# S5 branch of a hybrid stream step: real scans in a turning frame, and tables and coefficients made during the first projection

## The chip, the cores and the metric

One core of a Trainium2 chip runs the whole program. The metric is the device time of one execution in microseconds (us). The engines are PE (TensorE matmuls; PEld is its weight load), DVE (VectorE), ACT (ScalarE), POOL (GpSimd) and SP (SyncE, which here only issues DMAs; ACT issues DMAs too).

## The reference, cut to what matters

The kernel is one inference step of a two-layer encoder over a prompt of 16 + 2048 frames and 8 running streams of 16 frames. The part that the change touches is the S5 mixer of layer 0: 32 groups of 64 complex states, a diagonal recurrence, then a gelu and a gated linear unit (GLU).

```python
dt = jnp.exp(log_dt)[:, None]
mag = jnp.exp(lam_re * dt)
ab_re, ab_im = mag * jnp.cos(lam_im * dt), mag * jnp.sin(lam_im * dt)
...
bu_re = jnp.einsum('btgc,gpc->btgp', ug, bb_re)     # and bu_im
_, _, h_re, h_im = lax.associative_scan(_cplx_combine, (a_re, a_im, bu_re, bu_im), axis=1)
y = einsum(h_re, c_re) - einsum(h_im, c_im)
y = gelu(y.reshape(bsz, T, W_A) + d * uf)
y = y * jax.nn.sigmoid(y @ w_glu + b_glu)
```

The rest of layer 0 is an input projection `u @ ev_w_in`, a causal convolution with SiLU, an mLSTM and an output projection; layer 1 has its own projections, a retention and an RG-LRU.

## The kernel before, in words

All matmuls of the projections are done as three products of split operands (`mm3`, L109 to L113), since each fp32 operand is held as a high and a low part (`split`, L103: an ACT cast, then a DVE or POOL subtraction). The code is plain Python over tiles; a planner puts every engine's instructions into one order ahead of time. It goes by program order, but lets a later instruction pass an earlier one that is not ready. On the chip each engine then runs its list strictly in that order. A tile of a pool takes its buffers in program order among the tiles of the same name, and must wait until the last reader of the buffer's former tile is done; pools on the right side form a stack, so that a pool that is opened after another one is closed gets the same addresses, and its tiles wait for the last use of the tiles that lay there.

The phases follow one another:

- `phase_in0`: six token blocks `seq = (2, 3, 4, 5, 0, 1)`, each with 8 output tiles of 128 columns: 4 for the S5 input (`uas`) and 4 for its gate (`zst`). Small work is set between the blocks: after block i = 0 the parameters, after i = 1 `prep_ml` and `s5_open` (powers of the S5 transition, `s5pw`, and the coefficients `s5bp`, `s5b0`, `s5b1`, in the pools `s5keep` and `s5kb`), after i = 4 the first weights of the next phase (`w_first`: tiles `wfh` and `wfl`, opened on the right side after `s5kb`). Then `uas` goes to DRAM (`e.ua`).
- `phase_l0`: three thirds of the tokens. A third has for each of 8 slices m an x tile (matmul, ACT copy to `xb`, four convolution passes on DVE (L537, L539), SiLU (L408), later a small gate matmul `pg` (L414) into one accumulator, m = 0 first) and a z tile (SiLU only, L382). The first x tile of the first third, and it alone, takes its weights from `w_first`. After every second slice `values` makes the value rows (`vo`, L439). The generator `s5` is advanced by one step after each tile from the third on; in the last third the z tiles come after S5 has been run to its end.
- `s5`: per q of 8 (4 groups each) load `s5u`, make the coefficient tile `s5ba` (L690 to L695), transpose it and multiply (`s5ee`, the input of the recurrence, 129 chunks per group). Then the recurrence over the chunks: `advance` on odd chunks (L751 to L755), 64 dependent steps of five small operations (L764 to L768), `advance` again. Then `s5y`, per q: the output coefficients `s5ca` (L816 to L820, a third of it on POOL), a Toeplitz block `s5tz` that goes through DRAM (`s5kp`, L830 and L833) and the output matmuls (L844 to L848). Once the last third has begun (`loaded`), `s5g`: load the result `s5gy` from DRAM (L874, 32 DMAs), gelu (L876), and 8 GLU blocks.
- then `phase_mlstm`, `phase_out0`, and layer 1 in `phase_in1` and `phase_ret`.

The names that count below: the pool `s5kb` is closed in `s5` after the recurrence (L783), so that `w_first`, `s5a` and the rest lie below it.

Of the kernel before, what the change touches and what calls it, by code (L numbers as in the profile page):

```python
# [19 lines left out]
NSEQ = 8  # L20
# [182 lines left out]
def phase_in0(e):  # L203
# [6 lines left out]
    with P(e, "a_w") as wp, P(e, "a_sb", 2) as sb, PS(e, "a_ps") as ps:  # L210
# [37 lines left out]
        for i, bi in enumerate(seq):  # L248
# [306 lines left out]
def s5_open(e, ps):  # L555
# [5 lines left out]
    with P(e, "s5prm", side="right") as sb:  # L561
# [37 lines left out]
        pw = s5.pw = keep.tile([128, 2, G, 17], F32, name="s5pw")  # L599
# [4 lines left out]
        t1 = sb.tile([128, G, 16], F32, name="s5t1")  # L604
        t2 = sb.tile([128, G, 16], F32, name="s5t2")
        k = 1
        while k < 16:
# [24 lines left out]
        sh = [128, G, 16]  # L632
        cmul(v, dk[:, 0], dk[:, 1], (pw[:, 0, :, 0:16], pw[:, 1, :, 0:16]),
             (kap[:, 0, :, None].to_broadcast(sh), kap[:, 1, :, None].to_broadcast(sh)), t1, t2)
# [21 lines left out]
        for q in range(2):  # L656
            hr = sb.tile([128, 128], F32, name=f"s5hr{q}")
# [9 lines left out]
def s5_u(e, sb, q):  # L667

    ur = sb.tile([128, 2, 4, NCH], F32, name="s5u")
# [6 lines left out]
def s5(e, ps):  # L676
# [6 lines left out]
    with P(e, "s5a", side="right") as sb:  # L683
        for q in range(8):
            gs = slice(4 * q, 4 * q + 4)
            ur = s5_u(e, sb, q)
            ba = sb.tile([128, 4, 16, 16], F32, name="s5ba")
            tmp = sb.tile([128, 4, 16, 16], F32, name="s5tm")
            sh = [128, 4, 16, 16]
            v.tensor_tensor(ba, p.bp[:, 0, gs, :, None].to_broadcast(sh), p.b[0][:, gs, None, :].to_broadcast(sh),  # L690
                            op=OP.mult)
            v.tensor_tensor(tmp, p.bp[:, 1, gs, :, None].to_broadcast(sh), p.b[1][:, gs, None, :].to_broadcast(sh),
                            op=OP.mult)
            v.tensor_add(ba, ba, tmp)
            v.tensor_copy(p.bb[:, gs, :], ba[:, :, 15, :])  # L695
# [37 lines left out]
        yield  # L733

        a32 = sb.tile([128, 2, G], F32, name="s5a32")
        a1 = sb.tile([128, G], F32, name="s5c1", bufs=2)
        a2 = sb.tile([128, G], F32, name="s5c2", bufs=2)
        v.tensor_mul(a1, p.a16[:, 0], p.a16[:, 0])
        v.tensor_mul(a2, p.a16[:, 1], p.a16[:, 1])
        v.tensor_sub(a32[:, 0], a1, a2)  # L740
        v.scalar_tensor_tensor(a32[:, 1], p.a16[:, 0], 2.0, p.a16[:, 1], op0=OP.mult, op1=OP.mult)

        def advance(dst, src, n, g0):

            gs = slice(g0, g0 + G // 2)
            h = ee[:, gs, src:src + 2 * n - 1:2]
            d = ee[:, gs, dst:dst + 2 * n - 1:2]
            t1 = sb.tile([128, G // 2, n], F32, name="s5ba")
            t2 = sb.tile([128, G // 2, n], F32, name="s5tm")
            bc = lambda j, ph: p.a16[ph, j, gs, None].to_broadcast([h[ph].shape[0], G // 2, n])  # L750
            v.tensor_tensor(t2[UP], h[LO], bc(1, LO), op=OP.mult)  # L751
            v.tensor_tensor(t2[LO], h[UP], bc(1, UP), op=OP.mult)
            nc.gpsimd.tensor_tensor(t1, h, bc(0, slice(0, 128)), op=OP.mult)
            v.tensor_add(d, d, t2)
            v.tensor_add(d, d, t1)  # L755

        for g0 in (0, G // 2):
            advance(2, 1, PCH // 2, g0)
            yield
        for c in range(2, PCH + 1, 2):  # L760
            a1 = sb.tile([128, G], F32, name="s5c1", bufs=2)
            a2 = sb.tile([128, G], F32, name="s5c2", bufs=2)
            h = ee[:, :, c - 2]
# [19 lines left out]
    cls(e, "s5kb")  # L783
    with P(e, "s5y", side="right") as sb:

        pw = p.pw
        cp = sb.tile([128, 2, G, 17], F32, name="s5cp")
        v.tensor_copy(cp[UP, 0], pw[UP, 0])
        v.tensor_scalar(cp[LO, 0], pw[LO, 1], -1.0, None, op0=OP.mult)
        v.tensor_scalar(cp[UP, 1], pw[UP, 1], -1.0, None, op0=OP.mult)  # L790
        v.tensor_scalar(cp[LO, 1], pw[LO, 0], -1.0, None, op0=OP.mult)
# [1262 lines left out]
```

## Time and profile before

| | us |
|---|---|
| three runs | 3146.6, 3149.01, 3157.82 |
| median | 3149.01 |
| the profiled execution, its own time | 3155.99 |
| its span from the first to the last instruction | 3154.3 |
| PE busy in the span | 3008.8 (95%) |
| DVE busy | 1722.9 (55%) |
| ACT busy | 1058.0 (34%) |
| POOL busy | 902.6 (29%) |

All views below are of the profiled execution, with times counted from the start of its span. A view by stretches gives the busy time of each engine in a stretch; PEclk in it is the granted TensorE clock as a share of 2.4 GHz. A view of waits adds up the idle time of an engine before instructions of a line, under the name of what ended last. The timeline lists instructions with start and duration, and in brackets the idle time of the engine ahead of them.

### The profile page before, as it was taken

The numbers are of one execution on the slowest core, as the hardware profiler recorded it, in microseconds if no ns is written. First come the engines' busy times: TensorE is split into PE (matmuls) and PEld (weight loads), VectorE is DVE, ScalarE is ACT, GpSimd is POOL, SyncE is SP. The second block draws the span as 40 slices with busy tenths as digits, with TensorE's granted clock in tenths as the row PEclk, the third lists the DMA queues.
The fourth block names the chain that finished last, engine by engine and source line by source line (L and its number), as shares of the span: only waits on it lengthen the run. The fifth ranks groups of instructions, "written<-read, shape, count | busy, mean of one in ns | idle before, by whom it ended". The sixth has DMA issues, their size and how long they took to land.

```text
span 3154.3 us, 45102 instructions
## 1 busy us (share of the span) xinstructions
PE 3008.8 (95%) x17435; PEld 2721.3 (86%) x17435; DVE 1722.9 (55%) x3449; ACT 1058.0 (34%) x1860; POOL 902.6 (29%) x931
## 2 busy tenths in 40 slices
PE   8999978997999899999999999999999999999999
PEld 8999877997987787766799999999998897888887
DVE  4236797465446886143355666766620026665664
ACT  4223332335343343211224555555531112211221
POOL 6103424343325663111202111111110014433432
PEclk9999988998999999999999999999999999999999
DMA  6436433558453556755532111111122148544442
GB/s 213 117 84 202 127 117 115 156 166 178 145 156 119 160 153 181 232 187 172 157 132 73 51 51 51 50 49 49 47 83 76 52 152 247 141 119 133 137 124 74
DMA packets 444033, 396.35 MB, mean 126 GB/s; under 512 B 43401, under 2 KB 392785, under 8 KB 443818
## 3 DMA queue, kind: packets, MB, share of 16 engines
q1 hardware_dynamic: 333164, 268.13, 29.8%
q10 hardware_dynamic: 110654, 125.33, 11.9%
q8 instruction: 137, 2.24, 0.3%
q14 instruction: 78, 0.64, 0.1%
HBM read 262.12 MB, written 131.27 MB: 125 GB/s over the span
## 4 chain that ended last, share of the span: by engine, by line
PE 75%; DVE 15%; DMA 5%; issue 3%; ACT 2%; POOL 1%; SPq 0%; ACTq 0%; DVEq 0%; POOLq 0%
PE p_pm L112 8%; PE p_pm L113 8%; PE p_pm L111 8%; PE pm L111 4%; PE pm L112 4%; PE pm L113 4%; PE r_pm L112 4%; PE r_pm L113 4%; PE r_pm L111 4%; PE pa L111 3%; PE pa L112 3%; PE pa L113 3%; DVE p_d L1637 1%; DVE xc L539 1%; DMA m_rw<-d_grow 1%
## 5 line engine op out<-in xcount | busy, mean ns | idle before, releaser
L111 PE MATMUL p_pm<-pu,p_wh 128*128 128x384 f32 (+1 forms) x1568 | 512.1, 327 | 0.2 <-ACT pu L105 0.2
L112 PE MATMUL p_pm<-pu,p_wh 128*128 128x384 f32 (+1 forms) x1568 | 511.8, 327 | 0.0
L113 PE MATMUL p_pm<-pu,p_wl 128*128 128x384 f32 (+1 forms) x1568 | 511.3, 326 | 0.0
L111 PE MATMUL pm<-ub,wh 128*128 128x384 f32 (+1 forms) x1136 | 382.8, 338 | 12.7 <-ACT vo L439 9.8
L112 PE MATMUL pm<-ub,wh 128*128 128x384 f32 (+1 forms) x1136 | 381.0, 335 | 1.6 <-DVE ub L106 1.6
L113 PE MATMUL pm<-ub,wl 128*128 128x384 f32 (+1 forms) x1136 | 376.8, 335 | 0.0
L111 PEld LDWEIGHTS p_pm<-pu,p_wh 128*128 128x128 f32 x1568 | 294.2, 188 | 1.8 <-issue 1.2
L112 PEld LDWEIGHTS p_pm<-pu,p_wh 128*128 128x128 f32 x1568 | 294.6, 188 | 1.0 <-issue 0.8
L113 PEld LDWEIGHTS p_pm<-pu,p_wl 128*128 128x128 f32 x1568 | 294.5, 188 | 0.0
L111 PEld LDWEIGHTS pm<-ub,wh 128*128 128x128 f32 x1136 | 219.1, 193 | 18.6 <-ACT vo L439 10.3
L112 PE MATMUL r_pm<-rol,r_gh 128*128 128x512 f32 x544 | 218.1, 401 | 5.0 <-POOL rol L106 5.0
L112 PEld LDWEIGHTS pm<-ub,wh 128*128 128x128 f32 x1136 | 219.6, 193 | 3.0 <-DVE ub L106 2.1
L113 PEld LDWEIGHTS pm<-ub,wl 128*128 128x128 f32 x1136 | 218.7, 193 | 1.2 <-issue 1.1
L111 PE MATMUL r_pm<-roh,r_gh 128*128 128x512 f32 x544 | 217.7, 401 | 0.7 <-ACT p_o L1547 0.7
L113 PE MATMUL r_pm<-roh,r_gl 128*128 128x512 f32 x544 | 217.4, 400 | 0.8 <-DVE r_gl L106 0.8
L106 POOL TENSOR_TENSOR p_wl<-p_wr,p_wh 128x1024 fp32r<-128x1024 f32 x34 | 81.8, 2408 | 384.9 <-ACT p_wh L105 384.9
L106 POOL TENSOR_TENSOR wl<-wr,wh 128x1024 fp32r<-128x1024 f32 x47 | 120.3, 2560 | 246.5 <-ACT wh L105 217.5
L112 PEld LDWEIGHTS r_pm<-rol,r_gh 128*128 128x128 f32 x544 | 103.0, 189 | 25.3 <-POOL rol L106 5.4
L113 PEld LDWEIGHTS r_pm<-roh,r_gl 128*128 128x128 f32 x544 | 103.1, 189 | 22.6 <-DVE r_gl L106 1.3
L111 PEld LDWEIGHTS r_pm<-roh,r_gh 128*128 128x128 f32 x544 | 102.6, 189 | 21.8 <-ACT p_o L1547 1.2
L106 POOL TENSOR_TENSOR p_xcl<-p_xc,p_xch 128x384 fp32r<-128x384 f32 (+1 forms) x48 | 47.2, 982 | 245.3 <-ACT p_xch L105 209.3
L1637 DVE RECIPROCAL p_d<-p_d 128x384 f32<-128x384 f32 (+1 forms) x48 | 116.7, 2430 | 0.6
(716 smaller groups left out, 6805.7 us busy)
## 6 DMA issues: line engine op xcount, KB each, us to landing
wr<-in_ev_w_in_dram SPq DMA_DIRECT2D x47, 512.0 KB
p_wr<-in_od_w_in_dram SPq DMA_DIRECT2D x40, 512.0 KB
d_in<-p_o ACTq DMA_DIRECT2D x80, 192.0 KB
m_rw<-d_grow SPq DMA_DIRECT2D x18, 512.0 KB
s5u<-d_ua SPq DMA_DIRECT2D x32, 274.0 KB
d_v<-vo ACTq DMA_DIRECT2D x68, 128.0 KB
m_va<-d_v SPq DMA_DIRECT2D x17, 512.0 KB
d_h<-o_x ACTq DMA_DIRECT2D x17, 512.0 KB
```

What stands on the lines that cost most here:

```text
L106: (nc.gpsimd if pool else nc.vector).tensor_tensor(l, x, h, op=OP.subtract)
L111: nc.tensor.matmul(out, a[0], b[0], start=start, stop=False, **kw)
L112: nc.tensor.matmul(out, a[0], b[1], start=False, stop=False, **kw)
L113: nc.tensor.matmul(out, a[1], b[0], start=False, stop=stop, **kw)
L539: v.scalar_tensor_tensor(out, x(j), pc[:, m, cw + j:cw + j + 1], out, op0=OP.mult, op1=OP.add)
L1637: v.reciprocal(d[:, :n], d[:, :n])
```

## The change

The recurrence over chunks is complex: state times `a16` (a 16th power) plus input. The change turns the input of each chunk c by the phase of `a16` to the power -c, runs a real scan with the magnitude `m16` for each of the 32 groups, and turns the result back. For that it makes per group a table of 128 phases (`e.rot`) by repeated squaring (`s5_phasors`, 10 squarings of 10 operations) and doubling (`s5_coef`). The coefficient tiles `s5ba` and `s5ca` are made there too. Table and coefficients go to DRAM and are loaded back one step ahead of their use. `s5_coef` runs its first part (tables, `s5ba`) after block i = 2 of `phase_in0` and its second part (C coefficients, `s5ca`) after i = 3, where it also closes `s5kb`. The pool `w_first` is opened at i = 4 as before. `s5pw` moves from `s5keep` to `s5kb`. The 64 chunk steps, both `advance` passes and the coefficient work inside `s5` are gone. The loads of `s5gy` get a step of their own, ahead of the GLU weights and of gelu, and the operands of GLU block b + 1 are made ahead of the matmuls of block b. The generator has 10 steps before the output part instead of 17, and 3 GLU blocks instead of one are left for the run to the end.

```diff
                 s5_open(e, ps)
+                coef = s5_coef(e, ps)
+            if i in (2, 3):
+                next(coef)
             if i == 4:
                 fp = opn(e, "w_first", side="right")
...
-        pw = s5.pw = keep.tile([128, 2, G, 17], F32, name="s5pw")
+        s5_phasors(v, sb, kb, s5, csn, sn, mag, keep)
+        pw = s5.pw = kb.tile([128, 2, G, 17], F32, name="s5pw")
...
+def s5_phasors(v, sb, kb, s5, cs, sn, mag, keep):
...
+    pp = s5.pp = kb.tile([128, 2, ROT, G], F32, name="s5pp")
...
+    def square(oc, os_, c, s):
+        v.tensor_mul(t1, c, c)
+        v.tensor_mul(t2, s, s)
+        v.scalar_tensor_tensor(os_, c, 2.0, s, op0=OP.mult, op1=OP.mult)
+        v.tensor_sub(oc, t1, t2)
+        v.tensor_mul(t1, oc, oc)
+        v.tensor_mul(t2, os_, os_)
+        v.tensor_add(t1, t1, t2)
+        v.tensor_scalar(t1, t1, -0.5, 1.5, op0=OP.mult, op1=OP.add)
+        v.tensor_mul(oc, oc, t1)
+        v.tensor_mul(os_, os_, t1)
+    for _ in range(4):
+        square(c, s, c, s)
+    for j in range(1, ROT):
+        square(pp[:, 0, j], pp[:, 1, j], pp[:, 0, j - 1], pp[:, 1, j - 1])
...
+def s5_coef(e, ps):
...
+    with P(e, "s5co", side="right") as sb:
+        for g0 in range(0, G, 4):
+            gs = slice(g0, g0 + 4)
+            tb = sb.tile([128, 2, 4, 128], F32, name="s5tb")
+            t1 = sb.tile([128, 4, 64], F32, name="s5r1")
+            t2 = sb.tile([128, 4, 64], F32, name="s5r2")
+            v.tensor_copy(tb[:, :, :, 0], p.pp[:, :, 0, gs])
+            for j in range(ROT):
+                k = 1 << j
...
+                cmul(v, tb[:, 0, :, k:2 * k], tb[:, 1, :, k:2 * k], (tb[:, 0, :, 0:k], tb[:, 1, :, 0:k]), pk,
+                     t1[:, :, :k], t2[:, :, :k])
+            nc.scalar.dma_start(e.rot[g0 // 4], tb)
+    with P(e, "s5cb", side="right") as sb:
...
+            nc.scalar.dma_start(e.sba[q], ba)
+    yield
+    with P(e, "s5cc", side="right") as sb:
...
+            ca, tmp = x1(4, 17, 16), x2(4, 17, 16)
...
+            nc.scalar.dma_start(e.sca[q], ca)
+    cls(e, "s5kb")
+    yield
...
+        def scan(q, rt):
+            gs = slice(4 * q, 4 * q + 4)
+            h = ee[:, gs, 2:PCH + 1]
+            for turn in (v.tensor_sub, v.tensor_add):
...
+                v.tensor_tensor(t2[UP], h[LO], rt[LO, 1], op=OP.mult)
+                v.tensor_tensor(t2[LO], h[UP], rt[UP, 1], op=OP.mult)
+                v.tensor_tensor(t1, h, rt[:, 0], op=OP.mult)
+                turn(h, t1, t2)
+                if turn == v.tensor_sub:
+                    for g in range(4 * q, 4 * q + 4):
+                        d = ee[:, g, 1:PCH + 1]
+                        v.tensor_tensor_scan(d, p.m16[:, g:g + 1].to_broadcast([128, PCH]), d, 0.0, op0=OP.mult,
+                                             op1=OP.add)
+        nxt = loaded(0)
+        for q in range(8):
+            ur, ba, rt = nxt
+            if q < 7:
+                nxt = loaded(q + 1)
...
             yield
+            scan(q, rt)
...
-        for c in range(2, PCH + 1, 2):
...
-            v.tensor_tensor(a2[UP], h[LO], a32[LO, 1], op=OP.mult)
-            v.tensor_tensor(a2[LO], h[UP], a32[UP, 1], op=OP.mult)
-            v.tensor_tensor(a1, h, a32[:, 0], op=OP.mult)
-            v.tensor_add(a2, a2, ee[:, :, c])
-            v.tensor_add(ee[:, :, c], a1, a2)
...
+        nxt = toeplitz(0)
+        yield
+        for q in range(8):
+            ur, ca, tz = nxt
+            if q < 7:
+                nxt = toeplitz(q + 1)
...
+        gy = [sb.tile([128, 16, NCH], F32, name=f"s5gy{mt}") for mt in range(4)]
...
+                nc.sync.dma_start(gy[mt][16 * g:16 * g + 16], src[:, g])
+        yield
```

The pools `s5co`, `s5cb` and `s5cc` have one buffer per name (`s5tb`, `s5x1`, `s5x2`); the loads ahead (`s5u`, `s5ba`, `s5rt`, `s5ca`, `s5tz`) have two.

## Rows read from the trace of the kernel before

**Rows 1.** The page's part 1: busy time of PE and DVE.

```profile
PE 3008.8 (95%) x17435; PEld 2721.3 (86%) x17435; DVE 1722.9 (55%) x3449; ACT 1058.0 (34%) x1860; POOL 902.6 (29%) x931
```

**Rows 2.** Stretches of phase_l0: busy of each engine, PEclk, DMA share, GB/s.

```profile
247.00:340.00 93.00, 87.95 (x639) 84.89 (x638) 67.02 (x65) 39.99 (x84) 40.05 (x31) 0.98 0.63 193
340.00:550.00 210.00, 172.64 (x1061) 164.87 (x1060) 178.93 (x411) 64.73 (x120) 88.27 (x69) 0.89 0.38 115
550.00:745.00 195.00, 191.19 (x1313) 181.11 (x1312) 109.49 (x135) 75.25 (x141) 76.69 (x63) 0.99 0.55 165
745.00:800.00 55.00, 37.26 (x204) 34.61 (x204) 19.44 (x28) 30.18 (x47) 18.28 (x26) 0.75 0.91 159
800.00:905.00 105.00, 103.59 (x689) 101.09 (x688) 53.79 (x97) 32.54 (x71) 35.01 (x32) 1.00 0.54 176
```

**Rows 3.** Waits of PE, whole span: who for whom, us, times, longest.

```profile
PE pg L414 <- ACT xc L408: 31.0, 11, 6.5
PE pm L111 <- ACT vo L439: 9.8, 2, 9.5
PE s5p L778 <- DVE s5fin L775: 8.4, 1, 8.4
```

**Rows 4.** A chunk-step line, DVE, 340 to 550: busy, mean ns, idle before.

```profile
L766 DVE TENSOR_TENSOR s5c<-s5ee,s5a 128x32 f32<-128x32 f32 x63 | 20.8, 330 | 2.0
```

**Rows 5.** DVE timeline in s5_open: first rows of four complex multiplications, and the end.

```profile
171.23 0.22 DVE L543 TENSOR_TENSOR s5t<-s5pw 128x32 f32<-128x32 f32 x1
172.50 0.23 DVE L543 TENSOR_TENSOR s5t<-s5pw 128x64 f32<-128x64 f32 x1
173.82 0.29 DVE L543 TENSOR_TENSOR s5t<-s5pw 128x128 f32<-128x128 f32 x1
175.53 0.43 DVE L543 TENSOR_TENSOR s5t<-s5pw 128x256 f32<-128x256 f32 x1
178.04 0.21 DVE L617 TENSOR_TENSOR s5t<-s5lam 128x32 f32<-128x32 f32 x1
185.78 0.42 DVE L640 TENSOR_SCALAR s5bp<-s5dk 64x512 f32<-64x512 f32 x1
```

**Rows 6.** DVE timeline: wfl made, and the long gap behind it.

```profile
195.35 1.23 DVE L106 TENSOR_TENSOR wfl<-xt,wfh 128x1024 fp32r<-128x1024 f32 x1 [1.67 <-ACT wfh L105]
247.99 0.18 DVE L401 COPY xd<-pc 128x24 f32<-128x24 f32 x1 [49.93 <-DMA bif<-in_ml_b_if_dram]
```

**Rows 7.** Tiles s5ba and s5ca on DVE: duration ns min/median/max, first and last start.

```profile
L694 DVE TENSOR_TENSOR s5ba<-s5ba,s5tm x8: 1207/1212/1270, 263.8 to 352.4; 128x1024 f32<-128x1024 f32 x8
L816 DVE TENSOR_TENSOR s5ca<-s5cp,s5c x8: 1284/1291/2628, 531.3 to 713.8; 128x1088 f32<-128x1088 f32 x8
```

**Rows 8.** Timeline and chain: two stores of one-buffered tiles, until the buffer is free.

```profile
545.44 0.34 SPq L830 DMA_DIRECT2D d_kp<-s5kp  x1
548.68 0.15 DVE L822 MEMSET s5kp<- 128x112 f32 x1 [3.27 <-DMA d_kp<-s5kp]
...
247.48 6.45 DMA d_za<-zst
```

**Rows 9.** ACT timeline: an evacuation of 272 columns, and the first xb.

```profile
210.64 0.40 ACT L221 ACTIVATE zst<-pm 128x272 f32<-128x272 f32 x1 [2.60 <-PE pm L113]
249.97 0.39 ACT L384 COPY xb<-pm 128x272 f32<-128x272 f32 x1 [2.52 <-PE pm L113]
```

**Rows 10.** Tile s5ee on DVE: duration ns min/median/max, first and last start.

```profile
L764 DVE TENSOR_TENSOR s5c<-s5ee,s5a x64: 203/208/2393, 266.6 to 495.7; 64x32 f32<-64x32 f32 x64
L751 DVE TENSOR_TENSOR s5tm<-s5ee,s5a x4: 1220/1228/1237, 354.6 to 504.8; 64x1024 f32<-64x1024 f32 x2, 64x1040 f32<-64x1040 f32 x2
```

**Rows 11.** The scan of the RG-LRU on DVE: busy, mean ns, idle before.

```profile
L1654 DVE TENSOR_TENSOR_SCAN p_h<-p_d,p_th 128x128 f32<-128x128 f32 x8 | 3.4, 425 | 0.3
```

**Rows 12.** Waits of ACT, 745 to 800.

```profile
ACT s5gy L876 <- DMA s5gy<-d_ys: 9.2, 2, 4.6
ACT L876 <- DMA s5gy<-d_ys: 7.6, 1, 7.6
```

More of the change, by code (lines that the diff above doesn't have):

```diff
@@ L603, in s5_open @@
         v.tensor_mul(pw[:, 1, :, 1], mag, sn)
-        t1 = sb.tile([128, G, 16], F32, name="s5t1")
-        t2 = sb.tile([128, G, 16], F32, name="s5t2")
+        t1 = sb.tile([128, G, 8], F32, name="s5t1")
+        t2 = sb.tile([128, G, 8], F32, name="s5t2")
         k = 1
@@ L656, in s5_open @@
         for q in range(2):
-            hr = sb.tile([128, 128], F32, name=f"s5hr{q}")
+            hr = sb.tile([128, 128], F32, name="s5hr", bufs=1)
             for j, nm in enumerate(("re", "im")):
@@ L664, in s5_open @@
                           ph.rearrange("p q (s g) -> p q s g", s=4)[:, q])
-def s5_u(e, sb, q):
-    ur = sb.tile([128, 2, 4, NCH], F32, name="s5u")
+ROT = 7
+def s5_phasors(v, sb, kb, s5, cs, sn, mag, keep):
+    t1 = sb.tile([128, G], F32, name="s5q1")
+    t2 = sb.tile([128, G], F32, name="s5q2")
+    m16 = s5.m16 = keep.tile([128, G], F32, name="s5m16")
+    v.tensor_mul(m16, mag, mag)
+    for _ in range(3):
+        v.tensor_mul(m16, m16, m16)
+    pp = s5.pp = kb.tile([128, 2, ROT, G], F32, name="s5pp")
+    c, s = pp[:, 0, 0], pp[:, 1, 0]
+    v.tensor_copy(c, cs)
+    v.tensor_copy(s[UP], sn[UP])
+    v.tensor_scalar(s[LO], sn[LO], -1.0, None, op0=OP.mult)
+    def square(oc, os_, c, s):
[13 more added lines that the diff above has]
+        square(pp[:, 0, j], pp[:, 1, j], pp[:, 0, j - 1], pp[:, 1, j - 1])
@@ L670, in s5_u @@
+def s5_u(e, sb, q, bufs=1):
+    ur = sb.tile([128, 2, 4, NCH], F32, name="s5u", bufs=bufs)
     gs = slice(4 * (q % 2), 4 * (q % 2) + 4)
@@ L809, in s5, with toeplitz @@
                             d16[js, :, None].to_broadcast([16, 8, 16]), op=OP.mult)
[L810 to L820 removed]
+        def toeplitz(q):
+            ur = s5_u(e, sb, q, 2)
+            ca = sb.tile([128, 4, 17, 16], F32, name="s5ca", bufs=2)
+            nc.sync.dma_start(ca, e.sca[q])
             kp = sb.tile([128, 23, 16], F32, name="s5kp")
@@ L830, in s5 @@
             nc.sync.dma_start(e.kp[q], kp)
-            tz = sb.tile([128, 4, 16, 16], F32, name="s5tz")
+            tz = sb.tile([128, 4, 16, 16], F32, name="s5tz", bufs=2)
             for k in range(8):
@@ L858, in s5 @@
     with P(e, "s5g", side="right") as sb:
+        bg = sb.tile([128, 4], F32, name="s5bg")
+        r = e.row["s5"]
+        v.tensor_scalar(bg, e.pc[:, 4:8, r], 0.5, None, op0=OP.mult)
+        gy = [sb.tile([128, 16, NCH], F32, name=f"s5gy{mt}") for mt in range(4)]
+        for mt in range(4):
+            for g in range(8):
+                src = e.ys[mt].rearrange("h (t c) g n -> c g (h t) n", c=16)
+                nc.sync.dma_start(gy[mt][16 * g:16 * g + 16], src[:, g])
+        yield
         wg = []
@@ L865, in s5 @@
             wg += [[t[:, k] for t in wt] for k in range(2)]
[L866 to L869 removed]
         for mt in range(4):
[L871 to L875 removed]
+            yf = gy[mt].rearrange("p a b -> p (a b)")
             nc.scalar.activation(yf, yf, AF.Gelu_apprx_tanh)
[L877 removed]
+        yield
         flat = lambda t: t.rearrange("p a b -> p (a b)")
@@ L905, in s5 @@
             view, n, gs = nxt
+            if b < 7:
+                nxt = operands(b + 1)
             for mt in range(4):
@@ L1941, in scratch @@
     e.kp = dram.tile([8, 128, 23, 16], F32, name="d_kp")
+    e.rot = dram.tile([8, 128, 2, 4, 128], F32, name="d_rot")
+    e.sba = dram.tile([8, 128, 4, 16, 16], F32, name="d_sba")
+    e.sca = dram.tile([8, 128, 4, 17, 16], F32, name="d_sca")
     e.u = dram.tile([128, KD, T], F32, name="d_u")
```

144 lines of the change are left out of this document (57 added, 87 removed).

## The prediction

> **What bounds the kernel now.** I read the page first: PE is busy 95% of the span and DVE 55% [rows 1], so a change on DVE counts only where PE waits for it. The view by stretches then shows where PE has holes in phase_l0, the only phase in which S5 runs. From 247 to 905 us PE is busy 592.6 of 658 us, so it idles 65.4 us. Where the granted clock is under 1.00, PE was partly at the lower of its two levels (1.2 GHz against 2.4). A stretch with clock c and busy time b holds about (1 - c) * b of lost work: 1.8 + 19.0 + 1.9 + 9.3 = 32 us [rows 2]. Together that is 97 us, all that S5 can give back here; at full clock the PE work of the phase is 658 - 97 = 561 us. Of the 97 us, 56 lie in 340 to 550, where DVE is busy 179 of 210 us, and 27 in 745 to 800, where DVE is idle most of the time and the DMAs are busy. The waits name the owners: the gate matmuls waited 31 us for SiLU of tiles whose convolution stood in DVE's list between the chunk steps, the end of the recurrence cost 8.4 us, and the value matmuls lost 9.5 us in one piece [rows 3]. In that last place ACT itself was held 16.8 us by gelu waiting for its loads [rows 12].
>
> **What is removed, and the gain.** The chunk steps are 64 times five operations; one of these lines took 0.33 us on average between 340 and 550 [rows 4], another 0.208 us in the median and 2.4 us at worst [rows 10]. They and the two passes of `advance` leave DVE. What comes in their place per q is two turns, each of two products of 64x512, one of 128x512 and a sum of 128x512. A 64x1024 product took 1.22 us [rows 10], so 512 elements take 0.65 to 0.7 us, a turn 2.7 us. Four scans of 129 elements, at 0.425 us for 128 [rows 11], add 1.7 us. That is 7.2 us per q, in place of the 4 us for `s5ba` (three passes of 1.21 us and a copy [rows 7]) that leave the same step. A step of S5 costs PE about 10 us (a tile of 7.2 us, below, and S5's own matmuls), and DVE has its convolutions besides in every second step, so I take DVE as nearly full for eight steps and then nearly free. In 247 to 340, with DVE at 67 of 93 us, PE lost 5 + 1.8 us [rows 2]; I keep 14 us for the eight fuller steps. For the rest of the 97 us I keep 4 in the output part, 8 of the 27 at the gelu loads (they are still 32 DMAs, but ACT no longer stands behind them), and 4 for two more GLU blocks at the end. So 30 us stay, bounds 20 and 55, and the gain is 97 - 30 = 67 us.
>
> **What is added, and where it ends.** This part decides. The tables: in each of 8 passes seven complex multiplications of six operations, over 4 to 256 elements per partition. The trace has such chains back to back: 1.27 us from start to start at 32 elements (with a foreign operation in it, so 1.2), 1.32 at 64, 1.71 at 128, 2.5 at 256 [rows 5]. A pass is 4 * 1.2 + 1.32 + 1.71 + 2.5 = 10.3 us, eight are 83. `s5ba`: 8 * (3 * 1.21 + 0.2) = 31 us. `s5ca`: 8 * (3 * 1.29 + 0.6) = 36 us [rows 7], all on DVE now, POOL's third too. With two copies of C that is 151 us of DVE, outside the 100 small operations of the squarings.
>
> It can't start early. s5_open's chain ended at 186.2 [rows 5]; the squarings run beside it. Independent small operations start 0.11 to 0.14 us apart and dependent ones 0.2 to 0.25 us, so half of the squarings' 16 to 20 us is hidden and the tables start at about 194 (bounds 190 and 206). The tile `s5tb` lies on s5_open's scratch, so not sooner. DVE's free room in the projection is the gap up to 247.99 [rows 6]: 54 us, against 151.
>
> It can't run at DVE's pace either. `s5tb` and `s5x1` have one buffer each, so each of the 24 passes waits for the store of the one before. The nearest rows are a 184 KB store, 3.2 us from issue to a free buffer, and a 768 KB store next to other loads, 6.45 us [rows 8]. I take 4.0 us for 512 KB, nearer to the quiet one, since PE's loads stand still here; bounds 3.2 and 6.45. The Trainium skill ("DMA: Bandwidth & Descriptors", Anatomy of one DMA) gives 2.0 us plus the bytes at 436 GB/s; by it a 512 KB store would be an estimated 3.2 us, and the sum below 19 us shorter. The large row here is 2.6 us above that rule, the small one 0.8 us.
>
> So: tables 194 + 8 * (10.3 + 4.0 + 0.2) = 310. For `s5ba` one product is made while the store is under way: 8 * (2.5 + 4.0) + 1.2 = 53, to 363. C through one buffer twice, two loads and eight transposes: 8 us, to 371. `s5ca`: 7.9 for the first, 6 * 6.7, and 1.3 into the last: 420. With every store hidden it would be 194 + 151 = 345; at 6.45 us each, 420 + 24 * 2.45 = 479.
>
> Who waits for that? `s5kb` is now closed at i = 3, and `w_first`, 8 KB, is opened in its place. `s5kb` holds phases, powers, `s5bp`, `s5b0`, `s5b1`, in this order from below, and the last 8 KB are `s5bp` and the two `s5b`: `wfh` lies on `s5bp`, `wfl` on `s5b0` and `s5b1`, which hold C until the last `s5ca`. Today `wfl` is made at 195.35 [rows 6]; then it is made at 420 + 1.2, say 422 (bounds 346 and 481). The first x tile of phase_l0 needs it, and its first output was evacuated at 249.97 [rows 9], so PE is ready for it at 247. Behind it stand all gate matmuls (slice 0 opens their accumulator) and, since buffers of one name go out in program order, every later tile: while it holds two of four PSUM buffers and one of two `xc1`, only z0, x1 and z1 can pass. A tile is 24 matmuls of 272 columns, 3.0 us (an evacuation of 0.40 us behind a wait of 2.60 us [rows 9]), and as many of 384, 4.2 us by columns: 7.2 us. So three tiles fill 21.6 of the 175 us, and **PE idles 153 us more**. The planner does let later work pass (a chunk step ran at 266.6 us, 88 us before the `advance` that stands ahead of it in the program [rows 10]), but there is nothing more that has its buffers.
>
> **Edits at nothing.** 24 stores and 24 loads of 0.5 MB make 25 MB, in stretches with a DMA share of 0.38 to 0.55 [rows 2], and the loads are issued a step ahead; uncovered, each would cost one store time, 4 us. On ACT's queue the stores stand among the evacuations of the projection; a store that waits for DVE holds those behind it, at most the few us by which the list is off. S5's own start at about 426 instead of before 264 [rows 7] is hidden: eight steps of 10 and eight of 25 us end near 710, and the last third, for which the GLU waits anyway, begins after 800. POOL loses its part of `s5ca` and of `advance`; no wait of PE names it [rows 3].
>
> **The sum.** Start of the first tile 422 instead of 247, less 21.6 us done ahead, is +153; stalls 30 instead of 97 is -67; net +86 us. On the profiled 3156 that is 3242; the median lies 7 us lower, so **3235 us**. Bounds: 346 with 20 us of stalls gives 77 - 77 = 0, 3149; 481 with 55 gives 212 - 42 = +170, 3319.
>
> **Rivals.**
> - *The first tile isn't held* (faster). If `wfl` didn't lie on what the coefficients use, phase_l0 would start at 247 as today and the coefficients would run beside it on DVE, which is free 26 of 93 us there. S5 starts late but isn't waited for. Then only the gain counts, less some 10 us of convolutions behind table operations: 3149 - 67 + 10 = 3092 (3070 to 3125). For it: DVE's 50 us gap, and that the planner reorders. Against it: the stack. It turns at the point where the last `s5ca` ends: under 247 + 21.6 + 67 = 336 us the change gains; DVE's bare work says 345.
> - *The stores hide* or PE finds more to do than three tiles: an end of the coefficients at 345 to 380, or five more z tiles of 7.2 us. 3149 to 3184.
> - *Longer still*: stores at the upper row and ACT's list held in the projection, so that PE stalls before 247 too: 3320 to 3370.
>
> **How the numbers follow.** Forecast 0.63 (3184 to 3320); stores hidden 0.17, of which 0.10 is over 3165; not held 0.11; longer 0.09. The forecast and the second case hold 0.80, so the range is 3150 to 3320. A measurement of this kernel tells 0.5%, 16 us, from no change: slower 0.63 + 0.10 + 0.09 = 0.82, same 0.07, faster 0.11.
>
> **What would show it.** Right: in the timeline of PE a hole that begins near 247, with the first matmul on `wfl` at 380 to 480; DVE busy with L543 to L548 of the tables up to about 310, its gaps of 4 us ended by DMAs of `s5tb`; no long wait of L414 afterwards; phase_mlstm's first matmuls 70 to 110 us later than 905. Wrong: PE without a hole at 247, or `wfl` made before 300; a table pass much under 14 us; or stalls of the old kind in the steps with scans.

## The result, and the profile after

The changed kernel takes 3280.11 us (median of four runs, 3271.46 to 3284.23) against 3152.3 us for the kernel before in the same comparison: ratio 1.0401 with the interval 1.0386 to 1.0415, some 127 us slower. The forecast was 3235 us, range 3150 to 3320. The sign holds, and so does the main mechanism: PE stands still until the coefficients are made. The size is 45 us short, because the hole was larger and the gain smaller than forecast.

The profiled execution took 3281.55 us, its span 3279.7 against 3154.3 before: 125.4 us more. First the page of the changed kernel: busy time of the engines, and PE's row of the 40 slices.

```profile
PE 2998.9 (91%) x17435; PEld 2713.6 (83%) x17435; DVE 1782.4 (54%) x3698; ACT 1057.8 (32%) x1860; POOL 870.0 (27%) x919
PE   8990098998999999899999999999999999999999
```

PE does the same work as in [rows 1] in a longer span. Slices four and five are empty: 163 us in which PE has nothing to do but 2.2 us of transposes, more than the whole loss. DVE is busy 59.5 us more than before, although the slow recurrence is gone.

Waits of PE in the changed kernel, whole span (who for whom, us in all, times, longest):

```profile
PE s5p L754 <- DMA s5x<-in_s_c_re_dram: 120.1, 1, 120.1
PE pm L111 <- ACT wfh L105: 38.0, 1, 38.0
PE pg L417 <- ACT xc L411: 20.3, 5, 11.9
```

The timeline of PE at the end of the hole (start, duration, and in brackets the idle time ahead):

```profile
366.43 1.09 PE L754 MATMUL s5p<-ident,s5x 128*128 128x128 f32 x4 [120.08 <-DMA s5x<-in_s_c_re_dram]
...
409.68 0.59 PE L111 MATMUL pm<-ub,wfh 128*128 128x272 f32 x1 [38.03 <-ACT wfh L105]
...
410.93 0.43 PE L111 MATMUL pm<-ub,wh 128*128 128x272 f32 x1
...
413.65 0.29 PE L111 MATMUL pm<-ub,wh 128*128 128x272 f32 x1
...
414.69 0.39 PE L113 MATMUL pm<-ub,wfl 128*128 128x272 f32 x1
```

The hole is one stretch of 163 us (246.8 to 409.7) with two owners in series. For 120 us PE stands at the transposes of C (L754). They wait for a load of C into `s5x1`, which is free only after the last `s5ba` is stored. Then it stands 38 us for `wfh`. In [rows 3] the longest wait of PE is 9.5 us.

Stretches of the changed kernel (busy of each engine, PEclk, DMA share, GB/s), beside [rows 2]:

```profile
247.00:409.00 162.00, 2.17 (x8) 1.43 (x8) 116.91 (x308) 6.86 (x9) 6.46 (x5) 0.51 0.35 118
410.00:550.00 140.00, 130.01 (x924) 125.30 (x924) 110.85 (x143) 49.48 (x111) 46.43 (x40) 0.94 0.54 178
550.00:710.00 160.00, 153.23 (x1086) 143.87 (x1084) 53.92 (x62) 59.11 (x116) 46.30 (x40) 1.00 0.73 218
710.00:760.00 50.00, 33.70 (x186) 32.42 (x183) 7.25 (x6) 26.34 (x35) 17.40 (x20) 0.80 1.00 172
760.00:850.00 90.00, 84.41 (x518) 82.19 (x517) 44.98 (x50) 33.63 (x57) 36.02 (x29) 0.97 0.36 116
850.00:1037.00 187.00, 182.02 (x1214) 175.91 (x1212) 106.94 (x177) 72.40 (x145) 70.12 (x74) 0.99 0.51 160
```

The tiles of phase_l0 now run from 409.7 to 1036.4 us, 627 us. Before they ran from 246.8 to 909.5, 663 us. So the phase itself became 36 us shorter and starts 163 us later: +127, and no later phase moves against the next. By the sum of the prediction (idle time plus (1 - clock) times busy) PE still loses 10 + 7.8 us in 410 to 550, 6.8 in 550 to 710, 16.3 + 6.7 in 710 to 760 and 10.6 + 4.3 behind it: 62 us, where 30 were forecast.

Why the coefficients end when they do: the chain of work of the changed kernel (start, duration, what), a few of its pieces.

```profile
317.93 2.61 DMA d_rot<-s5tb
...
323.03 1.24 DVE s5x L738
324.29 2.61 DMA d_sba<-s5x
326.99 1.24 DVE s5x L734
328.25 1.24 DVE s5x L738
...
363.99 2.31 DMA s5x<-in_s_c_re_dram
...
```

Sum, store, product, sum: the single buffer puts DVE and DMA in turn, half of each period for the store; only one product of a step is made while the store is under way. The timeline of DVE has the start of the tables, one table that came late, and the end:

```profile
200.01 0.17 DVE L719 COPY s5tb<-s5pp 128x8 f32<-128x8 f32 x1
237.51 0.17 DVE L719 COPY s5tb<-s5pp 128x8 f32<-128x8 f32 x1 [14.91 <-DMA d_rot<-s5tb]
413.42 1.22 DVE L106 TENSOR_TENSOR wfl<-xt,wfh 128x1024 fp32r<-128x1024 f32 x1
```

`wfl` is made at 413.4; forecast was 422, and in [rows 6] it was 195.35.

### The profile page after: what moved, and what is told of

The parts are those of the page before. It is cut to its first block, busy times and chain, and to the rows that moved or that the text cites. A ratio compares the mean times of both kernels' runs of the same rounds, so it can differ in the third digit from the quotient of the medians.

```text
span 3279.7 us, 45403 instructions
## 1 busy us (share of the span) xinstructions
PE 2998.9 (91%) x17435; PEld 2713.6 (83%) x17435; DVE 1782.4 (54%) x3698; ACT 1057.8 (32%) x1860; POOL 870.0 (27%) x919
## 4 chain that ended last, share of the span: by engine, by line
PE 73%; DVE 15%; DMA 7%; issue 2%; ACT 2%; ACTq 0%; POOL 0%; SPq 0%; DVEq 0%; POOLq 0%
PE p_pm L112 8%; PE p_pm L113 8%; PE p_pm L111 8%; PE pm L112 5%; PE pm L111 5%; PE pm L113 5%; PE r_pm L112 4%; PE r_pm L113 4%; PE r_pm L111 4%; PE pa L111 3%; PE pa L112 3%; PE pa L113 3%; DVE p_d L1714 1%; PE pn L1363 1%; PE pc L1366 1%
## 5 line engine op out<-in xcount | busy, mean ns | idle before, releaser
L106 POOL TENSOR_TENSOR wl<-wr,wh 128x1024 fp32r<-128x1024 f32 x47 | 115.4, 2455 | 275.2 <-ACT wh L105 259.3
L106 POOL TENSOR_TENSOR p_wl<-p_wr,p_wh 128x1024 fp32r<-128x1024 f32 x34 | 81.8, 2407 | 386.0 <-ACT p_wh L105 373.7
L540 DVE TENSOR_SCALAR xc<-xb,pc 128x656 f32<-128x656 f32 (+2 forms) x24 | 48.5, 2022 | 169.8 <-ACT xb L387 169.8
```

The lines of the kernel that those rows point to most:

```text
L106: (nc.gpsimd if pool else nc.vector).tensor_tensor(l, x, h, op=OP.subtract)
L540: v.tensor_scalar(out, x(3), pc[:, m, cw + 3:cw + 4], pc[:, m, cb:cb + 1], op0=OP.mult, op1=OP.add)
```

## The experiments

All ratios are against the kernel before, run beside each kernel on the same chip. Spans and stretches are of profiled executions.

**1. Without the first weights' pool.** From the changed kernel; `w_first` is gone, and the first x tile loads its weights like any other.

```diff
-            if i == 4:
-                fp = opn(e, "w_first", side="right")
...
-        if (third, m, isz) == (0, 0, 0):
-            wh, wl = e.wf
-        else:
...
+        split(nc, wh, wl, wr, pool=True)
```

> The changed kernel without the pool w_first: the first x tile loads and splits its weights like all others, on addresses that the coefficients never use. Theory (the first tile is held by its weights, which lie on the coefficients' pool): the first matmul of phase_l0 moves from 409.7 to about 258, since loading and splitting the weights is now uncovered; the hole of 163 us is nearly gone and the time is 3130 to 3150. Rival (PE's own list: the transposes of C, for which PE stood idle 120 us, are ahead of every tile of phase_l0): the first tile starts when they are done, at about 372, only the second wait of 38 us is saved, and the time is 3242.

Measured: 3259.01 us, ratio 1.0355 (1.0338 to 1.0373). The wait for `wfh` is gone. PE's timeline of this kernel:

```profile
365.82 1.09 PE L742 MATMUL s5p<-ident,s5x 128*128 128x128 f32 x4 [119.49 <-DMA s5x<-in_s_c_re_dram]
...
370.56 0.58 PE L111 MATMUL pm<-ub,wh 128*128 128x272 f32 x1
```

The tiles start 39 us earlier, right behind the transposes, and the time falls by 21 us. So the place of the first weights, on which the prediction put everything, carries only the last 38 us of the hole. The first 120 us belong to the order of PE's own list. (Of the other 18 us, 12.9 are lost again in the waits for SiLU in front of the gate matmuls, which grow from 20.3 to 33.2 us. `s5ca` now runs on DVE beside the first convolutions; that this is why is argued, not shown.)

**2. C early.** From the changed kernel: C is loaded, transposed and kept in a pool of its own ahead of the tables. To fit, one product of `s5ba` is made in halves and one of `s5ca` in quarters, which makes the chain some 22 us longer (a step of `s5ba` takes 6.1 us instead of 5.2, one of `s5ca` 7.4 instead of 5.3).

```diff
+    kc = opn(e, "s5kc", side="right")
+    cc = [kc.tile([128, G, 16], F32, name=f"s5c{j}") for j in range(2)]
+    with P(e, "s5cr", side="right") as sb:
...
+                nc.tensor.transpose(pc[:, m, :], cr[:, m].rearrange("p a b -> p (a b)"), e.ident)
```

> The changed kernel with C loaded, transposed and kept in a pool of its own ahead of the tables (to make room, one product of s5ba is made in two halves and one of s5ca in four quarters, some 8 us more DVE in all). No transpose of C is left in PE's way, and the weights of the first tile lie no longer on C, only on s5bp and B, whose last reader is the last s5ba. If the hold is by tile addresses: the weights are split at about 365, three tiles (z0, x1, z1, 21.6 us) pass ahead of that, and the time is 3280 - 45 - 21 = 3214. If the pool as a whole holds (its last reader is s5cp of the last s5ca, near 412): only the three tiles are gained, 3259. If z0, x1 and z1 don't pass either: 3280 or more.

Measured: 3300.64 us, ratio 1.0492 (1.0471 to 1.0513). PE's longest wait in this kernel:

```profile
PE pm L111 <- ACT wfh L105: 188.0, 1, 188.0
```

With the transposes out of the way the hole is as long as in the changed kernel, plus what the edit adds to the chain. So each of the two holds keeps PE out by itself. `wfh` lies on `s5bp`, whose last reader is the last `s5ba`, done at about 381 us here; yet `wfh` was made at 434. ACT's timeline of this kernel:

```profile
389.53 44.52 ACTq L779 DMA_DIRECT2D d_sca<-s5x  x7
434.10 1.04 ACT L105 CAST wfh<-xt 128x1024 fp32r<-128x1024 f32 x1 [167.33 <-DVE s5x L778]
```

In ACT's list it stands behind seven stores of `s5ca`, each of which waits for DVE, and next to the last copies that read the powers, in the same pool, at 434.2. So the address alone is not the hold either: it would have let `wfh` go 53 us sooner. Whether the planner hands a pool on only as a whole, or put `wfh` there for another reason, the trace doesn't tell. The three tiles that could pass by the prediction didn't pass here either.

**3. The price of the coefficients.** From the changed kernel; it leaves out the arithmetic of the tables, `s5ba` and `s5ca`, with the loads and transposes of C, and stores zeros to the same 24 places in DRAM.

```diff
-            v.tensor_copy(tb[:, :, :, 0], p.pp[:, :, 0, gs])
...
-            nc.scalar.dma_start(e.rot[g0 // 4], tb)
+            nc.scalar.dma_start(e.rot[q].rearrange("p a b c -> p (a b c)"), zz[:, :1024])
+            nc.scalar.dma_start(e.sba[q].rearrange("p a b c -> p (a b c)"), zz[:, :1024])
+            nc.scalar.dma_start(e.sca[q].rearrange("p a b c -> p (a b c)"), zz)
```

> The changed kernel with the arithmetic of s5_coef left out (tables, s5ba, s5ca, the loads and transposes of C): a tile of zeros is stored to all 24 places in DRAM, so that everything that loads them runs as before. It prices the rest of the change by itself. Theory: no hole, and what is left is the gain that the stretch after the hole shows in the changed kernel, 663 - 627 = 36 us: 3152 - 36 = 3116. The gain of the prediction, 67 us, would give 3085. If the scans, not the coefficients, made the hole: over 3200.

Measured: 3136.94 us, ratio 0.9961 (0.9945 to 0.9978); no hole. It has one wait of its own: the 24 stores stand back to back in ACT's list, and an evacuation behind them held PE. The waits of PE and a part of ACT's timeline of this kernel:

```profile
PE pm L111 <- ACT zst L221: 17.4, 1, 17.4
```

```profile
201.54 0.33 ACTq L718 DMA_DIRECT2D d_rot<-s5zz  x1
...
213.75 1.21 ACTq L720 DMA_DIRECT2D d_sca<-s5zz  x1
...
230.43 1.27 ACT L221 ACTIVATE zst<-pm 128x272 f32<-128x272 f32 x4 [28.56 <-DMA d_sca<-s5zz]
```

So everything else in the change is worth 11.7 us as it ran, or at most 29 us without that wait, where the prediction credited 67. The coefficients cost the difference to the changed kernel, 3280 less 3137 or some 143 us.

**4. s5ba first, then the first weights, then the rest.** From the changed kernel: `s5ba` is made first, its pool closed, and `w_first` opened there, so that it lies on nothing that the tables or `s5ca` use; C, tables and `s5ca` follow. Phases, powers and C get pools of their own, and one product of `s5ca` is made in quarters as in 2.

```diff
-            if i == 4:
+            if i == 2:
...
                 fp = opn(e, "w_first", side="right")
...
+            nc.scalar.dma_start(e.sba[q], ba)
+    cls(e, "s5kb")
+    yield
```

> The changed kernel with another order of the coefficients: s5ba first, its pool closed, the weights of the first tile put there at once, then C, the tables and s5ca, which run beside phase_l0. Theory: the first matmul of phase_l0 is at 247 to 252, no hole; DVE gives the remaining 115 us of tables and s5ca between the convolutions, so S5 starts 100 us or more later in the phase than in the changed kernel; if that is hidden, 3116 to 3130, with half of DVE's extra work on the path 3175. Rival (what holds PE is DVE's load by the coefficients, wherever they stand): 3250 or more.

Measured: 3194.38 us, ratio 1.0148 (1.0133 to 1.0163). The transposes of C hold PE for 20.4 + 9.4 us, and the first tile starts at 278. Yet the kernel is still 46 us slower than before: the 31 us of the later start, 15 more, and the gain of the scans are all lost. S5's first step starts on PE at 545 us here, against 434 in the changed kernel, and later PE waits 15.0 us in one piece for the mLSTM's gates (L1053), whose chain on DVE comes behind the last GLU block. The forecast was 3116 to 3130 with that start hidden and 3175 with half of DVE's extra work on PE's path; the time is above both.

**5. Both holds gone.** From the changed kernel, with the edits of 1 and 2 together.

```diff
-            if i == 4:
-                fp = opn(e, "w_first", side="right")
...
+    kc = opn(e, "s5kc", side="right")
+    cc = [kc.tile([128, G, 16], F32, name=f"s5c{j}") for j in range(2)]
```

> The edits of a1 and a2 together: no pool w_first, and C transposed and kept apart ahead of the tables. Each alone left a hole (a1 119 us, a2 188 us). Theory (two holds beside each other, each enough by itself: the transposes of C in PE's list, and the pool of the first weights): with both gone PE goes on at about 258, the hole shrinks to some 10 us, and the coefficients run beside the tiles. S5 begins only when their pools are free, so part of the gain is lost: 3280 - 150 + 20 (products in halves) + 20 = 3170 (3140 to 3195). Rival (a third hold, or DVE's load by itself): a hole of over 50 us, 3220 or more.

Measured: 3222.14 us, ratio 1.0205 (1.0186 to 1.0224). The hole is 15.9 us. PE's timeline of this kernel:

```profile
262.80 0.60 PE L111 MATMUL pm<-ub,wh 128*128 128x272 f32 x1 [15.85 <-ACT wh L105]
```

Neither edit alone shortened the hold to this, both together did, so the two holds explain the hole. The time is above the range forecast for that (3140 to 3195). What came in its place is in the stretches of this kernel (columns as above):

```profile
246.00:420.00 174.00, 142.76 (x938) 136.81 (x937) 134.94 (x326) 54.52 (x94) 65.09 (x59) 0.89 0.51 161
420.00:660.00 240.00, 210.93 (x1302) 202.66 (x1301) 207.53 (x297) 86.81 (x170) 88.30 (x69) 0.93 0.55 186
850.00:1000.00 150.00, 99.25 (x642) 89.78 (x642) 65.82 (x143) 58.02 (x121) 40.59 (x47) 0.78 0.48 145
```

DVE is busy 342 of the 414 us from 246 to 660, PE loses 47 and 44 us there, and S5's first step starts at 567 us, 10 us behind the last of the coefficients, on whose pools its tiles lie. Its end comes late, too (the last gate product starts at 937 us, against 861 in the kernel before): 73 us of 150 are lost in 850 to 1000, among them waits of PE of 17.2 us for the mLSTM's gates and 15.1 us for one of its loads, both behind that end in the chain. So S5's start is not free to move, and of the 67 us by which this kernel is slower some 51 lie outside the hole.

**6. Two table buffers.** From the changed kernel.

```diff
-            tb = sb.tile([128, 2, 4, 128], F32, name="s5tb")
+            tb = sb.tile([128, 2, 4, 128], F32, name="s5tb", bufs=2)
```

> The changed kernel with two buffers for s5tb in place of one, so that a table is made while the one before is stored. DVE waited 32 us there for the stores (29.7 in 6 pieces for the next table, 2.7 for the first s5ba). Theory (PE stands still until DVE's chain of coefficients is through): both waits of PE end 32 us earlier, the first matmul on the first weights moves from 409.7 to about 378, and the time is 3248. Rival (the chain is bound by the stores' rate or by DVE's operations): under 10 us, 3270 or more.

Measured: 3267.81 us, ratio 1.0359 (1.034 to 1.0379). PE's timeline of this kernel:

```profile
396.03 0.59 PE L111 MATMUL pm<-ub,wfh 128*128 128x272 f32 x1 [38.03 <-ACT wfh L105]
```

The first tile comes 13.7 us earlier and the time falls by 12.3: inside the hole, a microsecond of the coefficient chain is very nearly a microsecond of the kernel. The stores don't hide, though: DVE still waits 18.5 us for `s5tb` (29.7 in the changed kernel), up to 9.9 us at once, because the tables' stores stand in ACT's list among the 32 stores of `d_ua` there.

**7. Whole rows for gelu, in the changed kernel.** The S5 result is stored by 64 stores of one group each, on SP's queue, in the order in which gelu reads it; four whole loads take the place of 32.

```diff
-                nc.scalar.dma_start(e.ys[q // 2, mh, :, 4 * (q % 2):4 * (q % 2) + 4, :], yst)
+                dst = e.ys[q // 2].rearrange("(g c) (h t) n -> h g t c n", c=16, h=2)[mh]
+                for g in range(4):
+                    nc.sync.dma_start(dst[4 * (q % 2) + g], yst[:, g])
...
-            for g in range(8):
-                src = e.ys[mt].rearrange("h (t c) g n -> c g (h t) n", c=16)
-                nc.sync.dma_start(gy[mt][16 * g:16 * g + 16], src[:, g])
+            nc.sync.dma_start(gy[mt], e.ys[mt])
```

> The changed kernel with the result of S5 stored in the order in which gelu reads it: 64 stores of one group each in place of 16, and 4 loads with 8.8 KB per partition in one piece in place of 32 loads on 16 partitions with pieces of 548 bytes. It tests the term of the sum that was 23 us where 8 were forecast: ACT stood 16.8 us in front of gelu for those loads, in both kernels. Theory: the loads take a few us each, ACT's waits fall under 6 us, PE's waits at 710 to 760 (11.9 for SiLU, 4.4 for the value rows) nearly go, and the time is 3280 - 15 = 3265. Rival (the DMA engines are full there with other transfers, share 1.00): 3275 to 3280.

Measured: 3276.73 us, ratio 1.0385 (1.0365 to 1.0405), 3 us below the changed kernel; the two intervals overlap. Stretches of this kernel, and ACT's longest wait in 500 to 780:

```profile
550.00:710.00 160.00, 147.18 (x1004) 137.91 (x1004) 49.89 (x56) 54.16 (x107) 44.40 (x39) 0.95 0.71 204
710.00:760.00 50.00, 42.27 (x261) 39.67 (x260) 14.49 (x13) 27.15 (x39) 18.96 (x19) 0.97 0.60 201
```

```profile
ACT s5yst L926 <- DMA d_ys<-s5yst: 45.0, 11, 8.9
```

The loss at gelu falls from 23 to 9 us, so those loads were its cause. In 550 to 710 it grows from 7 to 20, where ACT now waits for the stores of the one buffer `s5yst`. One wait was traded for another.

**8. Whole rows, in the kernel before.** The same edit alone on the kernel before.

```diff
-    e.ys = dram.tile([4, 2, 128, 8, NCH], F32, name="d_ys")
+    e.ys = dram.tile([4, 128, 16, NCH], F32, name="d_ys")
...
-                nc.scalar.dma_start(e.ys[q // 2, mh, :, 4 * (q % 2):4 * (q % 2) + 4, :], yst)
+                dst = e.ys[q // 2].rearrange("(g c) (h t) n -> h g t c n", c=16, h=2)[mh]
```

> The same edit of the stores and loads of S5's result in the kernel before, nothing else of the change. There the stretch 745 to 800 lost 27 us. Theory: 15 to 20 us of it are saved, 3130 to 3135, 0.5% under the kernel before. Rival (the loads were hidden, or 48 more stores take the place on SP's queue): 3145 to 3155.

Measured: **3138.52 us**, ratio 0.9951 (0.9934 to 0.9968): with experiment 12 the fastest complete kernel of this study, faster than the kernel before and the changed one. The stretch 730 to 800, the kernel before first, then this kernel:

```profile
730.00:800.00 70.00, 52.26 (x311) 49.03 (x311) 29.05 (x43) 37.11 (x60) 23.24 (x28) 0.80 0.87 162
```

```profile
730.00:800.00 70.00, 60.61 (x398) 57.07 (x398) 29.06 (x50) 42.08 (x72) 29.73 (x35) 0.90 0.50 169
```

The DMA share falls from 0.87 to 0.50, PE gains 8.4 us of work and a higher granted clock, and ACT's 16.8 us in front of gelu [rows 12] are gone. ACT waits 7.6 us for `s5yst` here, against 45 in experiment 7; that the slower output part is the reason is argued, not shown.

**9. Scans and tables alone.** From the kernel before: the scans take the place of the recurrence and only the tables are made ahead; `s5ba` and `s5ca` stay where they were. `w_first` is opened below the S5 pools and ahead of the tables, so nothing holds the first tile; the powers wait in DRAM for `s5y`.

```diff
+            if i == 2:
+                s5_tables(e)
...
+            scan(q, rt)
...
-        for c in range(2, PCH + 1, 2):
```

> The kernel before with the scans in the turning frame, but with only the tables made in the first projection: s5ba and s5ca stay where they were in S5, with C and their operands, and the weights of the first tile get a place below the S5 pools ahead of the tables, so that nothing of S5 lies under them (the powers wait in DRAM for s5y). Theory (what was wrong was the place of the coefficients, not the scans): no hole at 247; the tables run on beside the first tiles to about 340, S5's steps follow until about 460 against 515 before, and of the 29 us that a3 shows at most (3149 - 3137 + 17 of the stores of zeros), 10 to 25 are left: 3125 to 3140. Rival (the tables, 83 us of DVE, give back what the scans save): 3145 to 3165.

Measured: 3171.64 us, ratio 1.0054 (1.003 to 1.0079). No hole, and still no gain: the time is above both ranges. Stretches of this kernel, then one of the kernel before:

```profile
247.00:340.00 93.00, 78.77 (x515) 74.67 (x514) 82.00 (x228) 30.99 (x54) 34.48 (x35) 0.93 0.59 189
460.00:550.00 90.00, 78.47 (x465) 74.42 (x464) 57.95 (x73) 26.43 (x45) 36.69 (x29) 0.93 0.48 145
```

```profile
460.00:550.00 90.00, 70.80 (x409) 66.83 (x408) 74.92 (x166) 22.82 (x40) 39.05 (x29) 0.87 0.35 108
```

The scans give PE 7.7 us of work in 460 to 550. The tables take 9.2 us in 247 to 340, against [rows 2], with DVE up from 67 to 82 of 93 us. DVE's work was not only moved: over the whole span DVE is busy 1763.0 us, 40 more than in [rows 1], and S5's first matmul on its input runs at 361 us instead of 278. The two stretches make only 1.5 of the 17 us that this kernel is slower; the rest lies in smaller pieces that were not followed.

**10. Experiment 9 with whole rows** (the edit of 8), and two buffers of `s5yst`.

```diff
-                yst = sb.tile([128, 4, NCH], F32, name="s5yst")
+                yst = sb.tile([128, 4, NCH], F32, name="s5yst", bufs=2)
```

> c1 and the edit of b4 together (S5's result stored in the order in which gelu reads it), with two buffers for s5yst, since in b3 ACT waited 45 us for the stores of its one buffer. Theory: the two gains add up, the 16 us of b4 to that of c1, 3110 to 3125. Rival (as in b3, the stores take back in the output part what gelu gains): as c1, 3125 to 3140.

Measured: 3153.46 us against 3153.54, ratio 0.9998 (0.9988 to 1.0008): the 18 us of the whole rows do come on top of experiment 9, but from its slower start, so the time is above both ranges. This kernel is as fast as the kernel before, and 0.5% behind experiment 8, which has no scans.

**11. The GLU part alone.** On the kernel before: the loads of `s5gy` in a step of their own, gelu a step later, the operands of a block ahead of the matmuls of the last, as in the change.

```diff
+        gy = [sb.tile([128, 16, NCH], F32, name=f"s5gy{mt}") for mt in range(4)]
...
+        yield
...
+            if b < 7:
+                nxt = operands(b + 1)
             for mt in range(4):
```

> The kernel before with only the end of S5 taken from the changed kernel: the loads of s5gy in a step of their own, gelu a step later, the operands of GLU block b + 1 ahead of the matmuls of block b. The prediction gave this part 19 of the 27 us lost at 745 to 800. By the prediction's step (ACT no longer stands behind the loads): 3130 to 3135. By the trace of the changed kernel, where ACT waits the same 16.8 us in front of gelu: no change, 3145 to 3158.

Measured: 3147.46 us, ratio 0.9979 (0.9966 to 0.9993), some 6 us. ACT's waits of this kernel in 700 to 820:

```profile
ACT L878 <- DMA s5gy<-d_ys: 6.3, 2, 5.9
ACT s5gy L878 <- issue: 5.6, 1, 5.6
ACT s5gy L878 <- DMA s5gy<-d_ys: 4.1, 1, 4.1
```

Gelu still stands in ACT's list ahead of work that PE needs, and still waits 16.0 us: 10.4 for its loads, and 5.6 for which the profile names nothing ("issue").

**12. Whole rows with two half buffers.** Experiment 8 with `s5yst` as two tiles of two groups.

```diff
-                yst = sb.tile([128, 4, NCH], F32, name="s5yst")
...
+                    yst = sb.tile([128, 2, NCH], F32, name="s5yst", bufs=2)
```

> The kernel b4 (the kernel before with S5's result stored in the order in which gelu reads it) with s5yst as two buffers of half the size, in the same room, since in b4 ACT still waited 7.6 us for the stores of its one buffer. If these waits are on PE's path: 3130 to 3135. If they are covered: as b4, 3136 to 3142.

Measured: 3138.95 us, ratio 0.9958 (0.9942 to 0.9974), the same as experiment 8. In the kernel before the wait for `s5yst` is covered.

## Why the prediction was right or wrong

**The chain of the coefficients: right.** Forecast and trace, in us: start of the tables 194 and 200.0; their end 310 and 320.6; end of `s5ba` 363 and 363.6; C 371 and 372.4; `wfl` 422 and 413.4. Inside it, errors met. The store was taken at 4.0 us and took 2.6 (gaps of DVE 2.7 to 3.0 where nothing else was in the way), so that a period of `s5ba` is 5.2 us, not 6.5. The Trainium skill ("DMA: Bandwidth & Descriptors", Anatomy of one DMA) states, for DMAs issued by GpSimd, the fit from which the prediction took its estimated 3.2 us; these stores are issued by ACT. The measured 2.6 lies below it and decides. Against that, one table was stored late: its store stood behind stores of `d_ua` in ACT's list, which cost DVE 14.9 us in one gap. The prediction had asked only the reverse, whether a store that waits for DVE holds others ("at most the few us by which the list is off"). A table pass took 9.7 us, not 10.3. Of the signs that the prediction named, the hole from 247 and the first matmul on `wfl` (414.7, within 380 to 480) came; the end of the tiles moved by 127 us, though, where the mLSTM was to come 70 to 110 later, and one wait of 11.9 us in front of a gate matmul stayed, at gelu.

**Who is held: half right.** The prediction let z0, x1 and z1 pass and took off 21.6 us. None passed. PE's list was run strictly in order, and the transposes of C (which it counted, at 8 us, only as a load on the chain) stood in it ahead of every tile of phase_l0: they are a wait added to PE, and it didn't ask what was queued behind it. Experiments 1, 2 and 5 show two holds, either of which is enough. That the tiles had their weights is in the timelines: those of two later tiles were split by 261.4 us (POOL, L106, shown at the end), and the first matmuls on such weights, `wh`, ran at 410.9, ahead of those on `wfl` at 414.7, as soon as x0's first matmul had been issued. Why they had to wait for it in experiment 2 is argued, not shown: they take buffers of the same names in order, and x0's come first. This step is 21.6 us of the 40 between the forecast +86 and the measured +127; the earlier end of the chain gave back some 12 of it, and the smaller gain, below, is the other 32.

**The gain: mis-sized.** 30 us of stalls were to stay, and 62 did. In the steps with scans 18 stayed (14 forecast), so the gain there is as forecast: 56 to 18. In the output part 7 (4). At gelu 23 (8): that step of the prediction is wrong. ACT did stand behind the loads, for as long as before. ACT's waits of the changed kernel in 700 to 770, beside [rows 12]:

```profile
ACT L953 <- DMA s5gy<-d_ys: 9.2, 2, 6.7
ACT s5gy L953 <- DMA s5gy<-d_ys: 7.6, 2, 5.4
```

It is 16.8 us again. A generator step of their own moves the loads in the program, but the 32 loads, at a DMA share of 1.00, landed later than the work that stands between them and gelu was done. Experiment 11 measured the edit by itself at some 6 us, where 19 were credited, and experiments 7 and 8 showed the cause by taking the loads away. At the end 15 us stayed (4). Experiment 3 gives the whole gain once more, from the other side: at most 29 us, not 67.

**The rival of 3092 us: wrong in its own terms.** In the changed kernel "S5's own start is hidden" wasn't put to the test: tiles and S5 both start late, at 409.7 and 434 us. The rival took it over for a kernel without the hold ("S5 starts late but isn't waited for", so only the gain counts), and there it is wrong. Experiment 5 has a hole of 15.9 us, starts S5 at 567 us, waits for its end and takes 3222 us; experiment 9 has no hole and takes 3172. The prediction counted DVE's new work only where it stood in the hole. The ledger sums the lines of DVE that belong to recurrence, scans and tables. Removed: the chunk steps 90.8 us and `advance` 30.1, together 121. Added: scans and turns 76.4, tables 84.6, squarings 18.4, together 179. So DVE has 58 us more to do (the page says 59.5, with all other lines, among them 10.3 us of `s5ca` that POOL did before), next to a phase where PE waits for DVE already. In none of the places that were run was it free. Lines of DVE in the changed kernel, 160 to 760 (busy, mean ns of one, idle before):

```profile
L812 DVE TENSOR_TENSOR s5t<-s5ee,s5rt 128x512 f32<-128x512 f32 x16 | 20.7, 1291 | 0.2
...
L548 DVE TENSOR_TENSOR s5tb<-s5r,s5r 128x4 f32<-128x4 f32 (+6 forms) x56 | 15.2, 271 | 1.9
```

The six lines of the tables, of which the dearest stands here, cost 83 us, more than the 76.4 of all turns and scans.

## What to carry to other kernels

Ask of every moved instruction what stands behind it in the strict list of its own engine: eight transposes, 2.2 us of PE in all, ahead of a phase that doesn't need them, held PE for 120 us. Before work is moved to a "free" stretch of an engine, write the ledger of what is removed and what is added on it; here the faster recurrence brought more work than it took away, and three placements without the long hole all lost (1.0205, 1.0148, 1.0054). And look for the cheap cause first: 32 loads in front of gelu were worth 0.5% in the kernel before, while no placement of the scans that was run gained.

## What the runs showed of the hardware

DVE operations were stretched beside POOL's. DVE, then POOL, of the changed kernel in the hole:

```profile
256.74 2.44 DVE L547 TENSOR_TENSOR s5r<-s5tb,s5pp 128x128 f32<-128x128 f32 x1
259.21 2.31 DVE L548 TENSOR_TENSOR s5tb<-s5r,s5r 128x128 f32<-128x128 f32 x1
261.56 1.27 DVE L549 TENSOR_TENSOR s5r<-s5tb,s5pp 128x128 f32<-128x128 f32 x1
262.75 0.28 DVE L550 TENSOR_TENSOR s5r<-s5tb,s5pp 128x128 f32<-128x128 f32 x1
```

```profile
256.59 4.79 POOL L106 TENSOR_TENSOR wl<-wr,wh 128x1024 fp32r<-128x1024 f32 x2 [10.54 <-ACT wh L105]
261.34 1.34 POOL L106 TENSOR_TENSOR wvl<-wv,wvh 128x528 fp32r<-128x528 f32 x1
```

Of four operations of one size three took 2.44, 2.31 and 1.27 us, one beside each of POOL's three subtractions, and the fourth, behind them, 0.28. The Trainium skill ("SBUF — State Buffer", SBUF: two separate sides) has a rule for this: the pair of ports that the two engines share is locked for a whole instruction, and the other engine blocks; it holds for a DVE operation that reads two operands from SBUF while POOL reads SBUF too, as here. The trace agrees. In the tables, the coefficients, the turns and the scans of this kernel 15 operations took over 1.3 times the median of their kind, and each of them lies beside POOL operations for most of its time; but not every one beside POOL was stretched. This sizes a term of the prediction: 7.2 us per q for turns and scans is right by the medians (7.1), while the means make it 76.4 / 8 = 9.5 us.

Stores issued back to back get dear for the engine that issues them: the first of the 24 in experiment 3 took ACT's queue 0.33 us, those from the fourth on about 1.2 us each, and ACT's next evacuation waited 28.6 us.

In the hole the granted clock is 0.51 over the whole stretch, that is the lower level (1.2 GHz), while PE does nothing. The first matmuls of 272 columns behind it take 0.43 us, and from 413.65 on 0.29: the way back cost some 2 us, nothing beside the hole itself.
